# The last job of the first experts taken back tile by tile, and the exact low parts of the second mixer made on VectorE alone

## The chip, the core and the metric

The kernel runs on one core of a Trainium2 chip. The metric is the device time of one launch in microseconds (us), the median of several runs. The core has TensorE (PE, matrix products into PSUM), VectorE (DVE), ScalarE (ACT), GpSimd (POOL), and SyncE (SP), whose queue issues most transfers from HBM. Each engine works through its own list of instructions strictly in the order in which they were written, and waits at an instruction until the semaphores that it names are up.

## What is computed

A first network of two layers (attention and a feed-forward part each) turns 256 tokens of width 1024 into `x`; a second network of two layers follows. Cut to what matters here:

```
for i in range(2):                                   # second network
    hx = modulate(rmsnorm(x, ln1_g[i]), sh1, sc1)     # and hc from ctx
    yx, yc = mixer_ab(...) if i == 0 else mixer_cd(...)
    x = x + g1 * yx
    ...
    out = moe(tokens, ...)        # 32 experts, two per token
    ctx = ctx + g2c * out[:, :n_ctx]                  # layer 0 only
    x = x + g2 * out[:, n_ctx:]
```

The place of interest is the seam between the experts of layer 0 (512 tokens: 256 of `x`, 256 of `ctx`) and the mixer of layer 1 (window attention beside a pooling mixer).

## The kernel before

**Tiles.** The 512 tokens are four tiles of 128, counted `t4` = 0, 1 (of `X`) and 2, 3 (of `C`, the context). A tile's row of 1024 is handled in two halves of 512 columns.

**Experts.** `moe` runs jobs of two experts each. Per job PE multiplies the gathered tokens by gate and up weights (L1973), then the hidden by the down weights (L2017); ACT and DVE split the result `Y` into an exact high and low part (`split_T`, L417 and L418). `combine(t4, halves)` takes a job's result back to a tile: two products on PE (L2026), a multiplication by the gate from PSUM on DVE (L2036, into `tm`), and the addition to the stream, L2038, on GpSimd, or for the last job on DVE. For the last job the first halves of all four tiles are taken back inside `moe`; the second halves come in `tail`, which here is `MixerCD.begin`.

**Exact products.** A matrix product with a fp32 weight is made of three fast ones: `w` is split into `wh` (a copy in the short format, ACT, L300) and `wl` (the rest, a subtraction, L301). `Splits.emit` makes one such chunk of 128x1024; which engine subtracts is its field `engine`:

```
nc.scalar.activation(wh, w, AF.Copy)
self.engine.tensor_tensor(wl, w, wh.bitcast(F32), op=OP.subtract)
```

Tokens are split in the same way in `Normed.finish`: PE turns a tile (L478, eight transposes into two PSUM buffers), ACT scales and shifts the first four pieces (L486) and DVE the last four (L484), ACT copies the high part (L489, twice) and GpSimd subtracts (L490, twice).

**Begin of the second mixer.** `MixerCD.begin` takes the last job back, norms each tile and starts the queries. Per tile, `square` (ACT, L440), `root` (ACT, L386, after which DVE makes the reciprocal root, L397 to L402), `scale` (ACT, L437, half a tile, and DVE, L438, the other half), and `norm.need`, which is `finish`. `queries(t4, ...)` is a product of a tile with four chunks (L319 to L321, twelve matmuls for each half of the depth). `defer(n, f)` calls `f` after `n` ticks of the written order; nothing is decided at run time.

**Run of the second mixer.** `MixerCD.run` makes the queries' rotation (`gqa_q`, from ACT L583 to the transposes L1118 on PE), the keys (L1544), the pooling branch (`U`, copied by ACT at L1569 and used by PE at L1577) and attention units: logits on PE (L1172), row maximum and bias on DVE (L1178), exponentials on ACT (L1190). Chunks for the output product are split meanwhile (L300, L301).

**Order of transfers.** `pump` issues the weights of all stages in one fixed list on SP, one unit of 1 MB per free buffer; a unit's buffer is free when `consumed` is called behind its last reader. So the weights of the second experts (L227, L231) are fetched ahead until the buffers are full, and then follow PE's use of them.

Of the kernel before, what the change touches and what calls it, by code (L numbers as in the profile page):

```python
# [11 lines left out]
F32 = mybir.dt.float32  # L12
# [3 lines left out]
OP = mybir.AluOpType  # L16
# [111 lines left out]
def body(tc, d, dump=None):  # L128
    nc = tc.nc
    es = ExitStack()  # L130
    with es:
# [288 lines left out]
        class Normed:  # L420
# [50 lines left out]
            def finish(self, xn, t4):  # L471
                s, t = TILES[t4]
                ts = slice(t * 128, (t + 1) * 128)
                for k2 in range(2):
                    p = trp().rearrange("p (k t) -> p k t", k=4)
                    for kk in range(4):
                        k = 4 * k2 + kk
                        nc.tensor.transpose(p[:, kk], xn[:, k * 128:(k + 1) * 128], ident)  # L478
                    f = self.whole[s][:, 4 * k2:4 * k2 + 4, ts] if self.whole else self.wk.tile([128, 4, 128], F32, name="spl", bufs=2)
                    for kk in range(4):  # L480
                        k = 4 * k2 + kk
                        sc, sh = scl[:, self.l, 0, s, k:k + 1], modT[:, self.l, 0, k, s:s + 1]
                        if k2:
                            nc.vector.tensor_scalar(f[:, kk], p[:, kk], sc, sh, op0=OP.mult, op1=OP.add)  # L484
                        else:
                            nc.scalar.activation(f[:, kk], p[:, kk], AF.Identity, bias=sh, scale=sc)  # L486
                    if s in self.parts:
                        hi, lo = [h[:, 4 * k2:4 * k2 + 4, ts] for h in self.parts[s]]
                        nc.scalar.activation(hi, f, AF.Copy)  # L489
                        (nc.vector if k2 and t4 in self.ss else nc.gpsimd).tensor_tensor(lo, f, hi.bitcast(F32), op=OP.subtract)  # L490

            def __call__(self, k, t4):
                self.need(t4)
# [950 lines left out]
        class MixerCD:  # L1444
# [10 lines left out]
            def begin(self, combine):  # L1455

                norm, tiles = self.norm, (0, 1, 2, 3)
                there.clear()
                for p in self.rings:
                    del free[p]  # L1460
                norm.whole = [big(n, [128, 8, 256]).bitcast(F32) for n in ("lo0", "lo1")]
                xn = [big(n, [128, 2, D]).bitcast(F32) for n in ("hi0", "hi1")]
                norm.parts = {0: [self.rings[1].tile([128, 2048], F32, name="w").bitcast(F32R).rearrange("p (k t) -> p k t", k=8)
                                  for _ in range(2)]}
                st = {t4: norm.steps(streams[TILES[t4][0]][:, TILES[t4][1]], t4, xn[TILES[t4][0]][:, TILES[t4][1]]) for t4 in tiles}
                square, root, scale = [lambda t4, i=i: st[t4][i]() for i in range(3)]
                sp = self.sp = Splits(self.rings[0], end_moe[0], end_cd, 2, skip=(end_moe[0] + 2,), engine=nc.gpsimd)
                def joined(t4, between=lambda: None):
                    combine(t4)
                    between()  # L1470
                    square(t4)
                    root(t4)

                def one():
                    scale(0)
                    sp.emit()
                    norm.need(0)
                joined(0)
                joined(1, one)
                sp.emit()  # L1480
                scale(1)
                joined(2)
                sp.hold = True
                defer(2, lambda: norm.need(1))
                defer(3, lambda: scale(2))
                self.queries(0, lambda c, t, ps: self.first.append(ps))
                joined(3)
                sp.engine = nc.vector
                self.last = lambda: scale(3)

            def queries(self, t4, done):
# [4 lines left out]
            def run(self, right, more):  # L1496
                norm, sp = self.norm, self.sp
                with ExitStack() as inner:
# [36 lines left out]
                    def keys(tiles, j0):  # L1535

                        ps = []
                        w = units[end_moe[0] + 2]
                        for t4 in tiles:
                            norm.need(t4)  # L1540
                            p = acc()[:, 0:256]
                            s, t = TILES[t4]
                            for k in range(8):
                                nc.tensor.matmul(p, norm.whole[s][:, k, t * 128:(t + 1) * 128], w[:, k], start=k == 0, stop=k == 7)  # L1544
                                if k % 4 == 3:
                                    tick()
                            ps.append(p)
                        sp.hold = False
                        sp.resume(2)
                        if tiles[0] == 2:  # L1550
                            consumed(end_moe[0] + 2)
                            sp.engine = nc.gpsimd
                        gqa_kv(at, ps, tiles, self.tk, KT, V, j0, 5)

                    chain = lambda c, t, ps: gqa_q(at, ps, self.tq, QT, t, 4)
# [48 lines left out]

                    gone = []
                    sp.ended = gone.append
                    sp.engine = nc.vector
                    gated_out(sp, pl, parts, (0, 1), 0, [gate[:, :512]], lambda t4: None, KP)
                    drain()
                    on_tick.remove(beside)  # L1610
# [308 lines left out]
        def moe(l, route, u0, during, ending, tail):  # L1919
# [3 lines left out]
            with ExitStack() as ph:  # L1923
# [259 lines left out]
                jobs = list(range(NE // 2))  # L2183
# [30 lines left out]
                prev = None  # L2214
# [12 lines left out]
                for i, j in enumerate(jobs):  # L2227
                    cur = sides.pop(i)
                    loop = i == OVER + 2
                    if loop:  # L2230
                        tc.mark_branch_hint_location(f"left{l}", engines=[mybir.EngineType.PE])

                    def next_two():
                        sides.update((n, side(jobs[n])) for n in range(i + 1, min(i + 3, len(jobs))))
                        group = Group(list(sides.values())) if sides else None
                        if group:
                            group.match()
                        return group
                    if i % 2 and not loop:
                        group = next_two()  # L2240
                    nxt = sides.get(i + 1)
                    for m in range(2):
                        p = cur.project(m, u)
                        if i == 0 and m == 0:
                            route.weights()
                            cur.turn_P()
                            cur.weights()
                            route.windows(route.rk)
                            if EXTRA[l]:
                                ei, sl, w1 = route.pick(wk, route.none)  # L2250
                                extra.append((sl, w1))
                                wanted[l] = ei
                            route.right.close()
                            wr = ph.enter_context(tc.tile_pool(name=f"wrm{l}", bufs=1, side="right"))
                            gates = [gate_load(wr, l, 1, s) for s in range(NT // 2)]
                        cur.act(m, p)
                        if m == 0 and i + 1 == len(jobs):
                            ending()
                        if prev:
                            for t4 in order if loop and m == 0 else () if loop else order[m * half:(m + 1) * half]:  # L2260
                                prev.combine(t4)
                    cur.hidden_T()
                    if loop:

                        left_over()
                        group = next_two()
                        nxt = sides[i + 1]
                    elif nxt:
                        if i % 2:
                            group.gather()  # L2270
                        nxt.turn_P()
                    for n in range(2):
                        cur.down(n, u)
                        if nxt and n == 0:
                            if loop:
                                group.gather()
                                nxt.turn_P()
                            nxt.weights()
                        if i + 1 == len(jobs) and n:
                            for t4 in range(NT):  # L2280
                                cur.combine(t4, (0,), nc.vector)
                    if i == 0:
                        during()
                    u += cur.units
                    prev = cur
                tail(lambda t4: prev.combine(t4, (1,), nc.vector))

        def put(v, extra=False, whole=False):
            plan.append((v, extra, whole))
# [78 lines left out]
        end_moe = [plan_moe(0)]  # L2368
# [206 lines left out]
```

## Time and profile before

| | |
|---|---|
| median of 3 runs | 2161.28 us (2159.53 to 2161.49) |
| profiled execution, its own time | 2162.79 us |
| span in its profile | 2160.9 us |
| PE busy | 1988.7 us (92%) |
| DVE busy | 1034.2 us (48%) |
| ACT busy | 734.2 us (34%) |
| POOL busy | 398.8 us (18%) |
| SP's transfers, share of 16 DMA engines | 71.5% |
| HBM read | 607.90 MB, 283 GB/s over the span |

Busy shares are averages over very different stages: what bounds the kernel must be read stage by stage. Times in the rows further down are us from the span's start. A wait row names who waited, for whom, and then the total, the number and the longest of the waits. In a timeline row the columns are start, duration, engine, line, operation, what is written and read, the shape, how many were merged, and in brackets the idle time of the engine before it and who ended it.

### The profile page before, as it was taken

Reading aid. Unit: us, or ns where it says so; the run is one execution under the profiler, and the core shown is the slowest. Engines: PE = TensorE matmul, PEld = TensorE weight load, DVE = VectorE, ACT = ScalarE, POOL = GpSimd, SP = SyncE. Lnnn points to the kernel's source line nnn. Section 1 sums busy time; section 2 is a strip of 40 time slices with the busy share of each in tenths; the row PEclk is TensorE's granted clock in tenths of the full one; section 3 lists DMA queues with packets and bytes.
Section 4 is the critical chain, followed back from the end, with each engine's and each line's share of the span. In section 5 each row is a group of like instructions: output and inputs, shape, how many; then the busy total and the mean of one; then the engine's idle time right before and its main releaser. Section 6 shows DMA issues by size and latency. Waiting matters only on the chain. (4 is left out here: it accounts for less than half of the span.)

```text
span 2160.9 us, 28242 instructions
## 1 busy us (share of the span) xinstructions
PE 1988.7 (92%) x10991; PEld 1258.5 (58%) x10991; DVE 1034.2 (48%) x2123; ACT 734.2 (34%) x1287; POOL 398.8 (18%) x353
## 2 busy tenths in 40 slices
PE   7998999998999989677999999999788799998998
PEld 5765888775898878456444454445366444343333
DVE  5745555664667986967423333223553422221222
ACT  5544544555565456353111111111364311111110
POOL 3000110100110100014122333323420111111111
PEclk9999999999999999788999999999999899999999
DMA  9776677665465434105899998999552799999998
GB/s 326 280 253 224 236 254 265 222 251 199 159 203 186 163 119 139 45 25 200 329 421 417 411 412 349 400 413 416 197 205 78 299 420 421 420 421 401 407 421 339
DMA packets 160762, 612.96 MB, mean 284 GB/s; under 512 B 10527, under 2 KB 16255, under 8 KB 111344
## 3 DMA queue, kind: packets, MB, share of 16 engines
q1 hardware_dynamic: 155744, 596.86, 71.5%
q0 software_dynamic: 4448, 13.51, 2.2%
q8 instruction: 88, 1.44, 0.3%
q10 hardware_dynamic: 432, 0.74, 0.1%
q14 instruction: 50, 0.41, 0.1%
HBM read 607.90 MB, written 3.16 MB: 283 GB/s over the span
## 5 line engine op out<-in xcount | busy, mean ns | idle before, releaser
L1973 PE MATMUL acc<-w,XT 128*64 128x512 f32 x1856 | 432.4, 594 | 5.6 <-DMA w<-in_ex_gate_dram 3.4
L301 DVE TENSOR_TENSOR w<-w 128x1024 fp32r<-128x1024 f32 x244 | 297.5, 1231 | 170.2 <-ACT w L300 148.8
L300 ACT ACTIVATE w<-w 128x1024 fp32r<-128x1024 f32 x252 | 264.5, 1059 | 191.4 <-PE acc L321 91.7
L1973 PEld LDWEIGHTS acc<-w,XT 128*64 128x64 f32 x1856 | 136.9, 137 | 265.6 <-issue 239.4
L2036 DVE TENSOR_TENSOR tm<-acc,gate 128x512 f32<-128x512 f32 x196 | 129.5, 686 | 228.3 <-PE acc L2026 177.0
L2017 PE MATMUL acc<-w,hT 128*64 128x512 f32 x912 | 222.7, 613 | 14.0 <-PEq L2191 6.4
L2038 POOL TENSOR_TENSOR X<-X,tm 128x512 f32<-128x512 f32 x124 | 155.3, 1280 | 424.4 <-DVE tm L2036 424.4
L363 PE MATMUL acc<-hi,w 128*128 128x256 f32 x576 | 163.6, 284 | 5.4 <-ACT hi L489 2.2
L364 PE MATMUL acc<-lo,w 128*128 128x256 f32 x576 | 161.7, 281 | 0.8 <-POOL lo L490 0.8
L365 PE MATMUL acc<-hi,w 128*128 128x256 f32 x576 | 161.5, 280 | 0.0
L321 PE MATMUL acc<-w,lo 128*128 128x512 f32 x368 | 149.0, 405 | 1.3 <-POOL lo L1385 1.1
L319 PE MATMUL acc<-w,hi 128*128 128x512 f32 x336 | 141.6, 421 | 6.6 <-ACT hi L1384 5.3
L320 PE MATMUL acc<-w,hi 128*128 128x512 f32 x336 | 135.2, 402 | 8.2 <-DVE w L301 8.2
L2017 PEld LDWEIGHTS acc<-w,hT 128*64 128x64 f32 x912 | 64.1, 139 | 123.6 <-issue 110.5
L1999 ACT ACTIVATE hT<-trp 128x512 f32<-128x512 f32 (+1 forms) x33 | 19.5, 591 | 332.1 <-PE trp L1996 332.1
L2038 POOL TENSOR_TENSOR C<-C,tm 128x512 f32<-128x512 f32 x64 | 79.5, 1273 | 267.7 <-DVE tm L2036 267.7
L1990 DVE SCALAR_TENSOR_TENSOR hd<-sg,ws,acc 128x512 f32<-128x512 f32 (+1 forms) x33 | 36.3, 1099 | 168.7 <-issue 95.2
L363 PEld LDWEIGHTS acc<-hi,w 128*128 128x128 f32 x576 | 108.7, 189 | 7.9 <-ACT hi L489 2.6
L2154 PE MATMUL acc<-P,hi 128*128 128x256 f32 x544 | 103.5, 288 | 8.8 <-issue 6.5
L365 PEld LDWEIGHTS acc<-hi,w 128*128 128x128 f32 x576 | 110.1, 191 | 0.0
L364 PEld LDWEIGHTS acc<-lo,w 128*128 128x128 f32 x576 | 108.8, 189 | 1.5 <-POOL lo L490 1.1
L1317 DVE SCALAR_TENSOR_TENSOR cy<-GT,cols,cy 128x256 f32<-128x256 f32 x240 | 106.9, 502 | 0.3
(423 smaller groups left out, 3359.4 us busy)
## 6 DMA issues: line engine op xcount, KB each, us to landing
w<-in_ex_gate_dram SPq DMA_DIRECT2D x118, 1024.0 KB, 12.5
w<-in_ex_up_dram SPq DMA_DIRECT2D x118, 1024.0 KB, 13.6
w<-in_ex_down_dram SPq DMA_DIRECT2D x118, 1024.0 KB, 13.2
w<-in_ffn_w_dram SPq DMA_DIRECT2D x64, 1024.0 KB, 5.3
fw<-in_mod_w_dram SPq DMA_DIRECT2D x48, 1024.0 KB, 7.5
w<-in_a_w_qkv_dram SPq DMA_DIRECT2D x17, 1024.0 KB, 10.8
w<-in_w_in_ab_dram SPq DMA_DIRECT2D x14, 1024.0 KB, 5.2
w<-in_b_w_qkv_dram SPq DMA_DIRECT2D x12, 1024.0 KB, 5.7
```

The lines of the kernel that those rows point to most:

```text
L300: nc.scalar.activation(wh, w, AF.Copy)
L301: self.engine.tensor_tensor(wl, w, wh.bitcast(F32), op=OP.subtract)
L319: nc.tensor.matmul(ps[:, :n], xh, wh, start=first, stop=False)
L320: nc.tensor.matmul(ps[:, :n], xh, wl, start=False, stop=False)
L321: nc.tensor.matmul(ps[:, :n], xl, wh, start=False, stop=last)
L363: nc.tensor.matmul(z, wh[:, js], xh, start=k == 0 and j % 2 == 0, stop=False)
L364: nc.tensor.matmul(z, wh[:, js], xl, start=False, stop=False)
L365: nc.tensor.matmul(z, wl[:, js], xh, start=False, stop=k == 7 and j % 2 == 1)
L1973: nc.tensor.matmul(p[self.rows(a)], self.XT[:, 4 * k0 + k, self.rows(a)], units[v + a][:, k], start=k0 + k == 0, stop=4 * k0 + k == 7)
L2017: nc.tensor.matmul(self.p[c][self.rows(a)], self.hT[:, 2 * n + k, self.rows(a)], units[v + a][:, k, s], start=n + k == 0, stop=n + k == 2)
L2036: nc.vector.tensor_tensor(g, p, gates[s][:, c], op=OP.mult)
L2038: add.tensor_tensor(dst, dst, g, op=OP.add)
```

## The change

In the first experts the last job's first halves are no longer taken back inside `moe`; `joined(t4)` in the mixer's begin takes back both halves of a tile, then squares it. For tile 1 the scaling and turning of tile 0 stand between its two halves, and for tile 2 the scaling of tile 1 does. The first two weight chunks of the mixer are split after tile 0's square and root. All weight splits of the mixer (eight chunks that GpSimd subtracted) and the four token subtractions of tiles 0 and 1 are DVE's.

```diff
-                        (nc.vector if k2 and t4 in self.ss else nc.gpsimd).tensor_tensor(lo, f, hi.bitcast(F32), op=OP.subtract)
+                        (nc.vector if self.whole or k2 and t4 in self.ss else nc.gpsimd).tensor_tensor(lo, f, hi.bitcast(F32), op=OP.subtract)
...
-                sp = self.sp = Splits(self.rings[0], end_moe[0], end_cd, 2, skip=(end_moe[0] + 2,), engine=nc.gpsimd)
+
                 def joined(t4, between=lambda: None):
-                    combine(t4)
+
+                    combine(t4, (0,))
                     between()
+                    combine(t4, (1,))
                     square(t4)
                     root(t4)
...
                 joined(0)
+                sp = self.sp = Splits(self.rings[0], end_moe[0], end_cd, 2, skip=(end_moe[0] + 2,))
                 joined(1, one)
                 sp.emit()
-                scale(1)
-                joined(2)
+                joined(2, lambda: scale(1))
...
                 joined(3)
-                sp.engine = nc.vector
...
                             consumed(end_moe[0] + 2)
-                            sp.engine = nc.gpsimd
...
-                    sp.engine = nc.vector
...
-                        if i + 1 == len(jobs) and n:
+                        if l and i + 1 == len(jobs) and n:
...
-                tail(lambda t4: prev.combine(t4, (1,), nc.vector))
+                tail(lambda t4, halves=(1,): prev.combine(t4, halves, nc.vector))
```

What stands where on an engine moves with it. Lines of the changed kernel behind the edit are one lower, so its L2035 and L2037 are L2036 and L2038 of before. First DVE at the end of the last job, from the first product that comes back; `gate_9370` is the gate of `X`, `gate_9372` that of `C`. Before:

```order
L2036 TENSOR_TENSOR tm<-acc,gate_9370 128x512
L2038 TENSOR_TENSOR X<-X,tm 128x512
L2036 TENSOR_TENSOR tm<-acc,gate_9370 128x512
L2038 TENSOR_TENSOR X<-X,tm 128x512
L2036 TENSOR_TENSOR tm<-acc,gate_9372 128x512
L2038 TENSOR_TENSOR C<-C,tm 128x512
L2036 TENSOR_TENSOR tm<-acc,gate_9372 128x512
L2038 TENSOR_TENSOR C<-C,tm 128x512
L2036 TENSOR_TENSOR tm<-acc,gate_9370 128x512
L2038 TENSOR_TENSOR X<-X,tm 128x512
L2036 TENSOR_TENSOR tm<-acc,gate_9370 128x512
L2038 TENSOR_TENSOR X<-X,tm 128x512
```

And in the changed kernel, the same place as far as tile 0's reciprocal:

```order
L2035 TENSOR_TENSOR tm<-acc,gate_9370 128x512
L2037 TENSOR_TENSOR X<-X,tm 128x512
L2035 TENSOR_TENSOR tm<-acc,gate_9370 128x512
L2037 TENSOR_TENSOR X<-X,tm 128x512
L301 TENSOR_TENSOR w<-w 128x1024 x2
L2035 TENSOR_TENSOR tm<-acc,gate_9370 128x512
L2037 TENSOR_TENSOR X<-X,tm 128x512
L397 RECIPROCAL rstd<-sd 128x1
```

The four pairs ahead of tile 0's second half have become none, and two chunk subtractions and one pair now stand between tile 0's last addition and its reciprocal. Second, DVE between the scaling of tile 0 and that of tile 1 in the changed kernel, where before there were only the four L484:

```order
L301 TENSOR_TENSOR w<-w 128x1024
L490 TENSOR_TENSOR w<-lo,w 128x4x128
L484 TENSOR_SCALAR lo<-trp,scl,modT 128x128 x4
L490 TENSOR_TENSOR w<-lo,w 128x4x128
L2035 TENSOR_TENSOR tm<-acc,gate_9370 128x512
L2037 TENSOR_TENSOR X<-X,tm 128x512
L301 TENSOR_TENSOR w<-w 128x1024
L2035 TENSOR_TENSOR tm<-acc,gate_9372 128x512
L2037 TENSOR_TENSOR C<-C,tm 128x512
L397 RECIPROCAL rstd<-sd 128x1
```

Tile 1's second half, a chunk subtraction and tile 2's first half now all precede tile 1's reciprocal. Third, DVE at the first four attention units of the changed kernel; before, no L301 stood there:

```order
L301 TENSOR_TENSOR w<-w 128x1024 x3
L1178 ISA P,mx<-acc,w,rows 128x512
L1178 ISA mx 128x1
L1185 TENSOR_SCALAR low<-mx 128x1
L1178 ISA P,mx<-acc,w,rows 128x512
L1178 ISA mx 128x1
L1185 TENSOR_SCALAR low<-mx 128x1
L301 TENSOR_TENSOR w<-w 128x1024
L1178 ISA P,mx<-acc,w,rows 128x512
```

Three chunks now precede the first unit and one stands between the second and the third. ACT and PE change only in place: on ACT the first two L300 stand behind tile 0's square and root, and on PE the transposes of tile 0 stand ahead of three of the products that come back, while both products of tile 3 come back behind the queries of tile 0.

## Rows read from the trace of the kernel before

**Rows 1.** Windows: busy of PE, PEld, DVE, ACT, POOL; PE clock, DMA share, GB/s.

```profile
2100.00:2140.00 40.00, 36.62 (x155) 13.47 (x151) 6.59 (x11) 3.26 (x6) 7.50 (x6) 1.00 1.01 418
```

**Rows 2.** SP's own waits from 1500 us on.

```profile
SPq L227 <- PE acc L1973: 42.1, 18, 21.5
```

**Rows 3.** Timeline where the second experts begin, PE and SP.

```profile
1699.65 0.64 PE L1973 MATMUL acc<-C,XT 128*64 128x512 f32 x1
...
1703.33 0.33 SPq L227 DMA_DIRECT2D C<-in_ex_up_dram  x1
```

**Rows 4.** PE's waits between 1540 and 1720 us, the longest.

```profile
PE trp L478 <- ACT hi L437: 11.5, 1, 11.5
```

**Rows 5.** Timeline at the seam, tile 0, all engines.

```profile
1540.64 2.00 ACT L300 ACTIVATE w<-w 128x1024 fp32r<-128x1024 f32 x2
...
1541.38 0.68 DVE L2036 TENSOR_TENSOR tm<-acc,gate 128x512 f32<-128x512 f32 x1
...
1541.77 5.12 POOL L301 TENSOR_TENSOR w<-w 128x1024 fp32r<-128x1024 f32 x2 [5.12 <-ACT w L300]
...
1542.10 2.60 DVE L2038 TENSOR_TENSOR X<-X,tm 128x512 f32<-128x512 f32 x1
...
1545.33 2.12 DVE L2038 TENSOR_TENSOR X<-X,tm 128x512 f32<-128x512 f32 x1
...
1550.73 0.69 DVE L2038 TENSOR_TENSOR X<-X,tm 128x512 f32<-128x512 f32 x1
...
1552.96 0.17 DVE L397 RECIPROCAL rstd<-sd 128x1 f32<-128x1 f32 x1 [0.22 <-ACT sd L386]
...
1553.75 0.72 ACT L437 ACTIVATE hi<-X,rstd 128x512 f32<-128x512 f32 x1 [0.81 <-DVE rstd L402]
...
1554.52 1.97 PE L478 MATMUL trp<-cst,hi 128*128 128x128 f32 x8 [11.47 <-ACT hi L437]
...
1555.68 1.50 ACT L486 ACTIVATE lo<-trp,modT,scl 128x128 f32<-128x128 f32 x4 [0.26 <-PE trp L478]
...
1556.53 1.36 DVE L484 TENSOR_SCALAR lo<-trp,scl,modT 128x128 f32<-128x128 f32 x4 [2.30 <-PE trp L478]
1557.21 1.35 ACT L489 ACTIVATE w<-lo 128x512 fp32r<-128x512 f32 x2
```

**Rows 6.** L301 on DVE, 1500 to 1720 us: ns min/median/max, first and last start, form.

```profile
L301 DVE TENSOR_TENSOR w<-w x8: 1214/1220/1225, 1584.2 to 1663.8; 128x1024 fp32r<-128x1024 f32 x8
```

**Rows 7.** The same of L490 on DVE, in the whole span.

```profile
L490 DVE TENSOR_TENSOR lo<-spl,hi x2: 1340/1340/1341, 802.4 to 805.9; 128x512 fp32r<-128x512 f32 x2
```

**Rows 8.** Timeline, PE turns tile 1 and then tile 2.

```profile
1561.68 1.09 PE L478 MATMUL trp<-cst,hi 128*128 128x128 f32 x8
...
1571.90 1.03 PE L478 MATMUL trp<-cst,hi 128*128 128x128 f32 x8
```

**Rows 9.** Timeline, the queries of tile 0, from ACT to PE.

```profile
1571.76 0.58 ACT L583 ACTIVATE qr<-acc 128x512 f32<-128x512 f32 x1
...
1577.29 0.63 PE L1118 MATMUL trp<-cst,qr 128*128 128x128 f32 x4
```

**Rows 10.** Timeline of ACT at the first attention units.

```profile
1601.53 1.06 ACT L300 ACTIVATE w<-w 128x1024 fp32r<-128x1024 f32 x1 [0.27 <-ACT KT L1148]
...
1605.33 1.04 ACT L300 ACTIVATE w<-w 128x1024 fp32r<-128x1024 f32 x1
...
1608.21 0.59 ACT L1569 ACTIVATE U<-acc 128x512 f32<-128x512 f32 x1
```

**Rows 11.** Timeline of DVE in the same stretch.

```profile
1602.63 0.75 DVE L1178 CUSTOM_DVE_ANT_0 P<-acc,w,rows 128x512 f32<-128x512 f32 x1 [7.36 <-PE acc L1172]
...
1605.18 0.75 DVE L1178 CUSTOM_DVE_ANT_0 P<-acc,w,rows 128x512 f32<-128x512 f32 x1 [0.75 <-PE acc L1172]
```

**Rows 12.** Timeline of PE in the same stretch.

```profile
1605.57 0.60 PE L1577 MATMUL acc<-hi,U 128*128 128x256 f32 x2
...
1608.85 1.22 PE L1577 MATMUL acc<-hi,U 128*128 128x256 f32 x2 [2.68 <-ACT U L1569]
```

## Prediction

> **What bounds the kernel now.** The page's shares say that PE is 92% busy, which is a mean over stages, so the windows come first. Behind the seam, in the second experts, the DMA share is 1.01 at 418 GB/s [rows 1]: there the end is set by how soon the stream of weights gets going and by nothing that PE does later. So the question is what starts that stream. SP's own waits answer it: from 1500 us on its longest, 21.5 us, is for PE's first gate products, L1973 [rows 2]. The timeline shows the first of these at 1699.65 us and SP's next issue at 1703.33 [rows 3], so SP had stood with full buffers since about 1681.8. A product that frees a buffer later lets every later transfer start later, and no slack stands between. What delays the first L1973 by some us therefore delays the end by as many.
>
> Then I ask what sets that moment, and look at the seam. PE's longest wait there is 11.5 us, for ACT's scaling of tile 0 [rows 4], and the timeline of that stretch shows the chain before it: DVE brings back tiles, ACT squares, DVE makes the reciprocal, ACT scales, PE turns [rows 5]. The change works on that chain. It has to be added up tile by tile, since DVE now has all the subtractions of the begin in its one list.
>
> **Unit prices.** All from [rows 5] unless named. A pair (L2036 and L2038) is 0.72 to the start of the addition and 0.69 for one that nothing disturbs: 1.41. From the last addition's end (1550.73 + 0.69 = 1551.42) to the reciprocal is A = 1.54 (square and root). From there to ACT's scaling B = 0.79, to PE's transposes C = 0.77, from these to ACT's L486 D = 1.16, from that to the first L489 E = 1.53. One L489 is 0.68, the four L484 are 1.36. L300 is about 1.0 [rows 10], L301 on DVE 1.22 [rows 6]. L490 on these tiles has no row on DVE. Below, half of an L301 of twice its size is 0.61; above, 1.34 where it was DVE's in another stage [rows 7]. I take 0.69, the undisturbed addition of the same size and nearest in kind, and keep 4 x 0.65 = 2.6 us for the range.
>
> **Tile 0.** The four first pairs, of which two additions took 2.60 and 2.12 beside GpSimd, become one. DVE begins at 1541.38, and two pairs end at 1544.20. Were that all, the reciprocal would stand 7.2 us earlier. But in DVE's order two L301 and tile 1's first pair now precede it. Root ends at 1545.74, and only then does ACT make the first copy, until 1546.75. Two subtractions end at 1549.2, the pair at 1550.6, and with B and C PE turns tile 0 at 1552.15, against 1554.52: **2.4 us gained**.
>
> **Tile 1.** ACT has its first copied half of tile 0 at 1552.15 + D + E + 0.68 = 1555.5. DVE's list reads L490 (to 1556.2), L484 (1557.6), L490 behind the second copy at 1558.25 (1558.95), and only now tile 1's second pair (1560.35). Before, these subtractions were GpSimd's and the pair was done long ago. Root ends at 1561.9. Behind it ACT makes the third copy (1562.9), DVE its subtraction (1564.1) and tile 2's first pair (1565.5), and then the reciprocal that PE waits for. With B and C PE turns tile 1 at 1567.1 instead of 1561.68 [rows 8]: **5.4 us lost**, the gain gone and more.
>
> **Tiles 2 and 3, to the queries' rotation.** The scaling of tile 1 starts on ACT at 1566.3; DVE's half of it is taken as 0.5 (no row; not above ACT's 0.72). Tile 2's second pair ends at 1568.2, root at 1569.75. L486 of tile 1, ACT's next, takes it to 1571.3. Copies, L490, L484, copy, L490 follow as before (0.68, 0.69, 1.36, 0.68, 0.69): 1575.4, and tile 2's transposes stand at 1576.95 against 1571.90 [rows 8]. DVE then has the reciprocal (0.79), its half of the scaling (0.5) and both pairs of tile 3 (2.82): 1579.5. A, B and ACT's 0.72 of tile 3 come before the queries' L583: 1582.55 against 1571.76 [rows 9]. From L583 to the transposes L1118 were 5.53 us, which I keep, since the rotation is the same work: L1118 at 1588.1 against 1577.29, **10.8 us lost**. Before, 5.39 us went from tile 2's transposes to L1118, without a wait of note; counted from 1576.95 PE reaches L1118 at 1582.3 and stands there some 5.8 us. What covered DVE's extra work before was GpSimd's own list; that cover is gone.
>
> **The attention units.** Counted in the time of before. A copy starts at 1601.53 and ends at 1602.59 [rows 10]; its L301 is now DVE's and stands ahead of the first L1178, which came at 1602.63 [rows 11]. DVE had waited 7.36 us there, so the other subtractions are hidden, but this one ends at 1603.8: 1.2 lost. The fourth copy, at 1605.33 and pushed by the later exponentials to some 1606.2, ends near 1607.3; with L301 the third L1178 starts at 1608.5 instead of 1605.18: 3.3. ACT's copy of `U` at 1608.21 stands behind that unit's exponentials, and PE waits for this copy already, 2.68 us [rows 10, 12]. So **3.2 us** more are PE's.
>
> **PE's speed behind waits.** Behind that wait of 2.68 us the same pair of products took 1.22 instead of 0.60 [rows 12]. PE thus runs at half speed for a while behind a wait, and a wait of 5.8 us ahead of L1118 is new. How long such a while would last there no row shows: nothing below, some 3 us above (five such pairs); I take 1.5.
>
> By the Trainium skill ("TensorE: Matmul & The Clock Gate", Part 1), a PE that stood idle comes back at the low one of its two clocks; the halved pair agrees.
>
> **Sum.** 10.8 + 3.2 + 1.5 = 15.5 us. The profiled execution took 2162.79 us, 1.5 above the median, and becomes 2178.3; against the median of 2161.28 it is 2176.8, say 2177.
>
> **Rivals.** *Faster, because GpSimd lets go.* Two additions took 2.60 and 2.12 beside GpSimd's subtractions, 0.69 alone [rows 5]: 1.91 + 1.43 = 3.3 us of tile 0's path come back. If the rest of the seam follows tile 0, the gain is 2.4 (2158.9), and 7.2 (2154.1) if the two L301 move out of its way too. It is decided at tile 1: PE must turn it at or before 1561.68. Against it is DVE's list, where three subtractions and two foreign pairs now precede tile 1's reciprocal.
>
> The Trainium skill has the rule behind this ("SBUF — State Buffer", Who interferes with whom): DVE and GpSimd share a pair of ports under an exclusive lock, and the one that loses stands still. The long additions agree with it; by this rule alone the change would be a gain.
>
> *No change, because the transfers hide it.* The second experts run at the transfers' full rate, so a late seam could be made up: 2161.3. For it speaks the DMA share of 1.01; against it that SP stands 21.5 us with full buffers, ended by PE itself [rows 2, 3]. Nothing can be fetched ahead in that time.
>
> *Slower, but little.* If PE's waits overlap (its wait at the `U` copy may shrink as L1118's grows) and DVE's list is less stiff than added up, tile 1's 5.4 us is what stays: 2166.7.
>
> *Slower still.* The slow clock lasts over the whole stretch of attention, whose products PE then does more slowly between one wait and the next; with L490 at 1.34 us (2.6) and the clock at 3 us and more, 17 + 5 and above: over 2183.
>
> **How the numbers follow.** A change of 0.2%, 4.3 us, is about what can be told from none here. The forecast, a loss between 8 and 22 us, gets 0.80: it rests on sums of measured rows and on fixed lists. Faster 0.05, no change 0.04, the small loss 0.06, over 22 us 0.05. Below, the rotation's 10.8 without attention and clock gives 2172, and 2 to 3 less where waits overlap: 2169. Above, 2.6 for L490 and 1.5 more of the clock give 2181, with 2 for a loss of the same kind in the attention units: 2183. Outside lie the other cases, about 0.16 by their chances, and the ends of the forecast case. Faster 0.05, same 0.04, slower 0.91.
>
> **What would show it.** In the changed profile tile 0's transposes should start near 1552, tile 1's near 1567, tile 2's near 1577, L1118 near 1588 behind a PE wait for ACT of several us that was not there. L301 should be DVE's alone, at about 1.2 us, GpSimd's busy time lower, and the additions of tile 0 all near 0.69. The first L1178 should be about 12 us later, the third about 14, the first L1973 near 1715, and SP's wait for it longer by the same; behind it the DMA share unchanged. The prediction is wrong if tile 1's transposes come before 1562, if L1118 starts without a wait, or if L1973 is late and the end is not: then SP's buffers had slack that the waits don't show.

## The result and the profile after

The changed kernel takes 2175.25 us (median of 4 runs, 2172.06 to 2177.96), the kernel before 2161.24 beside it (2159.53 to 2161.49). The ratio is 1.0066, its 95% interval 1.0052 to 1.0081. That is 14.0 us slower, where 15.5 were forecast.

The page of the changed kernel gives its span, then busy time, share and number of instructions of each engine:

```profile
span 2174.3 us, 28225 instructions
...
PE 1995.8 (92%) x10991; PEld 1265.0 (58%) x10991; DVE 1041.3 (48%) x2135; ACT 735.2 (34%) x1287; POOL 374.4 (17%) x341
```

DVE did only 7 us more in all and POOL 24 us less. No share hints at a loss; it is one of place. The profiled execution took 2176.66 us, 13.9 more than the one before, and its span is 13.4 us longer. The two executions already differ ahead of the seam: the last split of `Y`, L418, starts at 1539.76 us here and at 1540.78 before, so from there on the changed kernel loses 14.4 us. All shifts below are counted from that L418. First PE, by its timeline through the seam (start, duration, idle time ahead and who ended it; L1545 is L1544 of before):

```profile
1550.85 1.97 PE L478 MATMUL trp<-cst,hi 128*128 128x128 f32 x8 [9.38 <-ACT hi L437]
...
1565.40 1.97 PE L478 MATMUL trp<-cst,hi 128*128 128x128 f32 x8 [7.58 <-ACT hi L437]
...
1574.87 1.10 PE L478 MATMUL trp<-cst,hi 128*128 128x128 f32 x8 [0.54 <-ACT hi L437]
...
1585.86 1.09 PE L1118 MATMUL trp<-cst,qr 128*128 128x128 f32 x4 [5.42 <-issue]
1586.74 2.85 PE L1545 MATMUL acc<-w,lo 128*128 128x256 f32 x8
1589.43 1.04 PE L478 MATMUL trp<-cst,hi 128*128 128x128 f32 x8
```

Tile 0's transposes are 11.09 us behind L418 instead of 13.74 [rows 5], a gain of 2.65. Tile 1's are 25.64 behind it instead of 20.90 [rows 8], a loss of 4.74, and PE, which had no wait there, now has one of 7.58. Tile 2's are 3.99 late, and L1118 9.59 [rows 9], behind a new wait of 5.42. DVE's timeline says why:

```profile
1539.76 0.69 DVE L418 TENSOR_TENSOR Yl<-acc,Yh 128x512 fp32r<-128x512 f32 x1 [1.05 <-ACT Yh L417]
...
1541.08 0.69 DVE L2037 TENSOR_TENSOR X<-X,tm 128x512 f32<-128x512 f32 x1
1541.69 0.68 DVE L2035 TENSOR_TENSOR tm<-acc,gate 128x512 f32<-128x512 f32 x1
1542.41 0.69 DVE L2037 TENSOR_TENSOR X<-X,tm 128x512 f32<-128x512 f32 x1
1545.70 2.36 DVE L301 TENSOR_TENSOR w<-w 128x1024 fp32r<-128x1024 f32 x2 [2.60 <-ACT w L300]
...
1554.21 0.69 DVE L490 TENSOR_TENSOR w<-lo,w 128x512 fp32r<-128x512 f32 x1 [1.21 <-ACT w L489]
1554.82 1.36 DVE L484 TENSOR_SCALAR lo<-trp,scl,modT 128x128 f32<-128x128 f32 x4
1556.88 0.69 DVE L490 TENSOR_TENSOR w<-lo,w 128x512 fp32r<-128x512 f32 x1 [0.70 <-ACT w L489]
1557.49 0.68 DVE L2035 TENSOR_TENSOR tm<-acc,gate 128x512 f32<-128x512 f32 x1
1558.21 0.69 DVE L2037 TENSOR_TENSOR X<-X,tm 128x512 f32<-128x512 f32 x1
1561.38 1.23 DVE L301 TENSOR_TENSOR w<-w 128x1024 fp32r<-128x1024 f32 x1 [2.49 <-ACT w L300]
```

Ahead of tile 0's second pair (1541.69) stands one pair now, its own first; the section on the change says none, the prediction counts it. The subtractions are short, but DVE stands idle ahead of nearly each of them, for ACT's copy: 2.60, 1.21, 0.70, 2.49 us. Tile 1's second pair, whose product PE had ended at 1553.7, stands at 1557.49 behind two of these waits. At the attention units DVE and then PE show:

```profile
1612.54 1.22 DVE L301 TENSOR_TENSOR w<-w 128x1024 fp32r<-128x1024 f32 x1 [0.36 <-ACT w L300]
1613.68 0.74 DVE L1178 CUSTOM_DVE_ANT_0 P<-acc,w,rows 128x512 f32<-128x512 f32 x1
...
1617.30 1.23 DVE L301 TENSOR_TENSOR w<-w 128x1024 fp32r<-128x1024 f32 x1 [1.83 <-ACT w L300]
1618.44 0.74 DVE L1178 CUSTOM_DVE_ANT_0 P<-acc,w,rows 128x512 f32<-128x512 f32 x1
```
```profile
1622.11 1.22 PE L1577 MATMUL acc<-hi,U 128*128 128x256 f32 x2 [5.49 <-ACT U L1569]
```

The third L1178 and PE's second pair on `U` are both 14.28 us late [rows 11, 12], and the wait of 2.68 has become 5.49. From there the loss passes almost unchanged to the end in this pair of profiles. SP's waits and its timeline, and a window of the second experts (busy of PE, PEld, DVE, ACT, POOL; clock, DMA share, GB/s):

```profile
SPq L227 <- DVE mx L1178: 42.5, 1, 42.5
SPq L227 <- PE acc L1972: 39.1, 17, 21.8
```
```profile
1694.51 0.42 SPq L227 DMA_DIRECT2D lo<-in_ex_up_dram  x1
1716.80 0.33 SPq L227 DMA_DIRECT2D C<-in_ex_up_dram  x1
```
```profile
2110.00:2150.00 40.00, 37.48 (x161) 13.55 (x159) 7.71 (x13) 3.86 (x7) 6.38 (x6) 1.00 1.01 421
```

SP's issue that had been at 1703.33 [rows 3] comes at 1716.80, 14.49 late by the same count, and the rate behind it is that of before [rows 1].

### The profile page after: what moved, and what is told of

Its sections match the earlier page's. It is cut to its first block, busy times and chain, and to the rows that moved or that the text cites. A ratio compares the mean times of both kernels' runs of the same rounds, so it can differ in the third digit from the quotient of the medians.

```text
span 2174.3 us, 28225 instructions
## 1 busy us (share of the span) xinstructions
PE 1995.8 (92%) x10991; PEld 1265.0 (58%) x10991; DVE 1041.3 (48%) x2135; ACT 735.2 (34%) x1287; POOL 374.4 (17%) x341
## 5 line engine op out<-in xcount | busy, mean ns | idle before, releaser
L301 DVE TENSOR_TENSOR w<-w 128x1024 fp32r<-128x1024 f32 x252 | 308.4, 1236 | 184.9 <-ACT w L300 163.4
L300 ACT ACTIVATE w<-w 128x1024 fp32r<-128x1024 f32 x252 | 264.5, 1059 | 193.9 <-PE acc L321 93.4
L2035 DVE TENSOR_TENSOR tm<-acc,gate 128x512 f32<-128x512 f32 x196 | 129.5, 685 | 235.4 <-PE acc L2025 184.3
L2037 POOL TENSOR_TENSOR X<-X,tm 128x512 f32<-128x512 f32 x124 | 155.2, 1279 | 424.3 <-DVE tm L2035 424.3
L2016 PE MATMUL acc<-w,hT 128*64 128x512 f32 x912 | 216.6, 602 | 8.5 <-ACT hT L1998 5.8
L2037 POOL TENSOR_TENSOR C<-C,tm 128x512 f32<-128x512 f32 x64 | 79.5, 1273 | 266.3 <-DVE tm L2035 266.3
## 6 DMA issues: line engine op xcount, KB each, us to landing
w<-in_ex_up_dram SPq DMA_DIRECT2D x118, 1024.0 KB, 14.4
```

The lines of the kernel that those rows point to most:

```text
L2016: nc.tensor.matmul(self.p[c][self.rows(a)], self.hT[:, 2 * n + k, self.rows(a)], units[v + a][:, k, s], start=n + k == 0, stop=n + k == 2)
L2035: nc.vector.tensor_tensor(g, p, gates[s][:, c], op=OP.mult)
L2037: add.tensor_tensor(dst, dst, g, op=OP.add)
```

## The experiments

**Theory.** Each subtraction that is moved to DVE waits for a copy of ACT, and DVE's list is strictly in order, so it makes the next tile's pairs and the row maxima wait too. **Rivals:** the tile-by-tile order itself does it, with another tile's work between a tile's halves; or DVE simply has too much to do; or sharing with GpSimd costs as much as it relieves.

The table holds all runs. Shifts are those of one profile, in us against the kernel before: the start of the row less the start of the last L418, less the same before (tile 0 13.74, tile 1 20.90, L1118 36.51, third L1178 64.40, SP's issue 162.55, end 620.12 behind L418). Ratios are to the kernel before.

| kernel | tile 0 | tile 1 | L1118 | third L1178 | SP's issue | end | ratio (95%) |
|---|---|---|---|---|---|---|---|
| changed | -2.65 | +4.74 | +9.59 | +14.28 | +14.49 | +14.42 | 1.0066 (1.0052 to 1.0081) |
| order_only | -6.22 | -1.13 | -0.03 | -0.06 | -1.60 | -1.78 | 0.9989 (0.9974 to 1.0004) |
| engines_only | -1.05 | +2.82 | +6.30 | +11.09 | +11.36 | +11.20 | 1.0061 (1.0037 to 1.0085) |
| keys_gpsimd | -2.64 | +4.74 | +9.55 | +10.99 | +10.75 | +10.70 | 1.0039 (1.0025 to 1.0053) |
| tokens_gpsimd | -2.65 | +1.94 | +4.57 | +9.59 | +8.45 | +8.41 | 1.0031 (1.0019 to 1.0043) |
| low_later | -2.63 | +1.47 | +6.29 | +11.69 | +9.19 | +9.26 | 1.0042 (1.0027 to 1.0056) |
| begin_gpsimd | -6.21 | -0.18 | +5.93 | +11.63 | +10.21 | +10.20 | 1.0051 (1.0036 to 1.0065) |
| rotation_first | -6.21 | -1.14 | -0.67 | -0.67 | -2.01 | -1.97 | 0.9995 (0.9985 to 1.0004) |
| square_later | -6.22 | -1.12 | -0.27 | -0.27 | -1.66 | -1.62 | 0.9996 (0.9987 to 1.0005) |
| tokens_first | -6.22 | -0.91 | +1.24 | +2.91 | +1.55 | +1.57 | 1.0010 (1.0001 to 1.0019) |

**The two halves of the change.** `order_only` is the changed kernel with its engine edits undone; `engines_only` is the kernel before with only these made:

```diff
-    (nc.vector if self.whole or k2 and t4 in self.ss else nc.gpsimd).tensor_tensor(lo, f, hi.bitcast(F32), op=OP.subtract)
+    (nc.vector if k2 and t4 in self.ss else nc.gpsimd).tensor_tensor(lo, f, hi.bitcast(F32), op=OP.subtract)
...
-    sp = self.sp = Splits(self.rings[0], end_moe[0], end_cd, 2, skip=(end_moe[0] + 2,))
+    sp = self.sp = Splits(self.rings[0], end_moe[0], end_cd, 2, skip=(end_moe[0] + 2,), engine=nc.gpsimd)
...
     joined(3)
+    sp.engine = nc.vector
...
     consumed(end_moe[0] + 2)
+    sp.engine = nc.gpsimd
...
     sp.ended = gone.append
+    sp.engine = nc.vector
```

> The tile-by-tile order of the change alone, every subtraction on the engine of the kernel before. Theory (the loss comes from the subtractions that stand in DVE's list, the order by itself frees tile 0): tile 0's transposes near 1549 to 1551, tile 1's no later than the 1561.7 of before, L1118 one to three us earlier than 1577.3, time 2157 to 2161 us. Rival (the order itself does it, since work of the tile before now stands between a tile's two halves): tile 1's transposes at 1565 or later and 2168 us or more.

> The order of the kernel before, all subtractions of the second mixer on DVE. Theory: tile 0 gains little, the rows of L301 and L490 that stand ahead of the next tile's additions make L1118 some 7 us late, the attention units add 3.3, together 2170 to 2173 us. Rival (the order does it): at most the 3.3 of the attention units, 2164 to 2165 us.

The engines are the loss (+11.2 us at the end), and the order is not: alone it loses nothing at any row of the table. So the rival of the order falls. The halves are no sum in the seam, though: at L1118 -0.03 and +6.30 stand against +9.59 together, at the third L1178 -0.06 and +11.09 against +14.28. The order puts tile 1's second pair behind tile 0's L490; with GpSimd these hold nobody up on DVE, with DVE they do. `engines_only` came near its numbers up to the third L1178, but its median of 5 is 2175.45 us beside 2163.68 of the kernel before, above the 2170 to 2173 expected. Its profile is of the fastest of these executions (2170.15). In time it can't be told from the changed kernel (ratios 1.0061 and 1.0066): the 3 us that the order adds to the engines are shown in the seam alone.

The rows of the seam repeat well: tile 1 is 4.74 late in both kernels that have the same begin, the changed one and `keys_gpsimd`. Behind it, from the third L1178 to SP's issue, the eleven profiles took 95.65 to 98.42 us at a granted clock of 0.86 to 0.89. So the last two columns of the table hold differences of up to 2.8 us that don't come from the seam.

One number missed: in `order_only` L1118 came no earlier. Of the 6.22 us that tile 0 gained, 1.13 is left at tile 1. PE's waits and DVE's and POOL's timelines there:

```profile
PE acc L321 <- POOL w L490: 3.0, 2, 2.4
PE trp L1118 <- issue: 2.8, 1, 2.8
```
```profile
1550.39 2.06 DVE L2040 TENSOR_TENSOR X<-X,tm 128x512 f32<-128x512 f32 x1
...
1554.13 0.13 DVE L390 TENSOR_SCALAR nv<-ss 128x1 f32<-128x1 f32 x1
1554.24 1.05 DVE L400 TENSOR_TENSOR sd<-rstd 128x1 f32<-128x1 f32 x1
1555.32 2.30 DVE L401 SCALAR_TENSOR_TENSOR sd<-sd,nv 128x1 f32<-128x1 f32 x1
1557.66 0.16 DVE L402 SCALAR_TENSOR_TENSOR rstd<-sd,rstd 128x1 f32<-128x1 f32 x1
```
```profile
1551.86 3.41 POOL L490 TENSOR_TENSOR w<-lo,w 128x512 fp32r<-128x512 f32 x2
1555.23 2.38 POOL L301 TENSOR_TENSOR w<-w 128x1024 fp32r<-128x1024 f32 x1
```

Beside GpSimd's subtractions DVE's steps take long, even those on 128 numbers: L401 ends when GpSimd's L301 does, 2.30 us where L402 takes 0.16. L2040, L400 and L401 stand on tile 1's way to its transposes and together take 4.4 us more than undisturbed (0.69, 0.16, 0.16), of the 5.1 that are lost between the two tiles. And L1118 waits 2.8 us for a rotation that stands behind tile 3 on ACT and DVE.

**The parts of the engine change.** Each kernel undoes one of the edits of the diff above in the changed kernel: the chunks from the keys on (its last two lines), the tokens (its first two), or the begin's four chunks (`Splits` with GpSimd, and DVE behind `joined(3)`).

> The changed kernel, but the weight chunks from the keys to the output product are GpSimd's again, as before. Theory: L1118 stays late by 9 to 10 us, and the first and the third L1178 both come 10 to 11 us later than before instead of 11.1 and 13.3; time 2171 to 2173 us against 2175. Rival (the copy of U waits for something other than these subtractions): no difference from the changed kernel, 2175.

> The changed kernel, but the four L490 of tiles 0 and 1 are GpSimd's again, as before. Theory (an L490 in DVE's list holds what stands behind it until ACT has copied, so it costs its wait and not its 0.69 us): tile 1's transposes come 2 to 3 us earlier than in the changed kernel, L1118 some 6 earlier, time 2167 to 2170 us. Rival (only DVE's busy time counts): at most 4 x 0.69 = 2.8 us come back, 2172.5 or more.

> The changed kernel, but the four weight chunks of the begin are GpSimd's again; tokens and later chunks stay on DVE. Theory: tile 0's transposes come as early as with the order alone (3.5 us ahead of the changed kernel), tile 1's 5 to 7 earlier than in the changed kernel, L1118 still 4 to 5 later than before since the L490 remain in DVE's list, and the attention units add their 3.3 us: 2168 to 2171 us. Rival (sharing with GpSimd slows DVE's additions by as much as its list is relieved): 2174 or more.

`keys_gpsimd` is as the theory has it: PE's second L1118, the first L1178 and the third are all 10.99 us late, so nothing is lost between them and the attention's 3.3 us are gone. The row of the third:

```profile
1619.97 0.75 DVE L1178 CUSTOM_DVE_ANT_0 P<-acc,w,rows 128x512 f32<-128x512 f32 x1 [0.75 <-PE acc L1172]
```

It waits for PE again, as before [rows 11], and not for a subtraction. `tokens_gpsimd` gives 2.80 us back at tile 1 and 5.0 at L1118 (6 were expected), more than the 2.8 us that four L490 keep DVE busy. Its median was 2170.19, just above the upper edge. `begin_gpsimd` gives tile 0 3.56 and tile 1 4.92 us back, a hair under the 5 expected; L1118 stays 5.93 late, 1 to 2 more than expected, and the time was 2171.97, also 1 us above. At the third L1178 it is 2.65 us earlier than the changed kernel, so GpSimd's subtractions relieve DVE's list by more than their sharing costs; its ratio, 1.0051 against 1.0066, doesn't tell the two apart. No part alone is the loss: at the third L1178 they give 3.3, 4.7 and 2.7 us back, of the 14.3 that lie between the changed kernel and `order_only`.

**The place in the list.** The same instructions on the same engines, and two of them moved:

```diff
-    (nc.vector if self.whole or k2 and t4 in self.ss else nc.gpsimd).tensor_tensor(lo, f, hi.bitcast(F32), op=OP.subtract)
+    if self.whole and t4 == 0:
+        self.low.append(lambda lo=lo, f=f, hi=hi: nc.vector.tensor_tensor(lo, f, hi.bitcast(F32), op=OP.subtract))
+    else:
+        (nc.vector if self.whole or k2 and t4 in self.ss else nc.gpsimd).tensor_tensor(lo, f, hi.bitcast(F32), op=OP.subtract)
...
+    norm.low = []
     joined(1, one)
+    for f in norm.low:
+        f()
```

> The changed kernel with the same instructions on the same engines; only the two L490 of tile 0 stand behind tile 1's second addition in DVE's list instead of ahead of it. Theory (it is the place in the in-order list that costs, since an L490 makes all behind it wait for ACT's copy): tile 1's transposes come 2.5 to 3 us earlier than in the changed kernel, the first product of the second experts 2 to 4 earlier, time 2171 to 2173 us. Rival (DVE simply has too much to do): no more than 0.5 us, 2175.

DVE's timeline of this run (L2041, L2043 and L491 are L2035, L2037 and L490 of the changed kernel):

```profile
1552.70 1.36 DVE L484 TENSOR_SCALAR lo<-trp,scl,modT 128x128 f32<-128x128 f32 x4
1553.97 0.68 DVE L2041 TENSOR_TENSOR tm<-acc,gate 128x512 f32<-128x512 f32 x1
1554.69 0.69 DVE L2043 TENSOR_TENSOR X<-X,tm 128x512 f32<-128x512 f32 x1
1555.30 1.29 DVE L491 TENSOR_TENSOR w<-lo,w 128x512 fp32r<-128x512 f32 x2
```

No wait is left among these, and tile 1's transposes come 3.27 us earlier than in the changed kernel, at the same amount of work on each engine. Some 1.9 us of it are the two waits that are gone (1.21 and 0.70), 1.2 the time of the two L490, which now lie where DVE would wait for ACT. That it is DVE's amount of work alone falls with it. At the third L1178 2.6 us remain of this gain. At the end it is 5.2, more than expected (the median is 2170.70), and the rest came later, on PE. From its second pair on `U` to SP's issue the two runs have the same long waits of PE but another clock:

```profile
1622.11:1716.80 94.69, 76.83 (x455) 56.06 (x457) 42.03 (x131) 45.24 (x90) 9.27 (x6) 0.87 0.36 136
```
```profile
1618.97:1711.26 92.29, 74.48 (x455) 54.60 (x457) 42.10 (x131) 45.41 (x91) 9.27 (x6) 0.90 0.37 141
```

The first is the changed kernel, the second `low_later`: 2.4 us shorter with a granted clock of 0.90 instead of 0.87, and about as much less of PE's busy time for the same 455 records. `order_only` gained its 1.5 us behind the third L1178 in the same stretch. One profile of each can't say whether that belongs to a kernel or to an execution.

**Towards a faster kernel.** On `order_only` the rotation was written ahead of tile 3's scaling, then tile 3's square was moved behind the rotation too, then GpSimd's L490 of tile 0 went ahead of its third chunk:

```diff
-    self.last()
     Spot(lambda shape: self.hold.tile(shape, F32, name="C"))
     chain(0, 0, self.first[0])
+    self.last()
...
-    joined(3)
+    combine(3, (0, 1))
-    self.last = lambda: scale(3)
+    self.last = lambda: (square(3), root(3), scale(3))
...
     scale(0)
-    sp.emit()
     norm.need(0)
+    sp.emit()
```

> The order of the change with the engines of before, and the rotation of tile 0's queries written ahead of tile 3's scaling. Theory (in the run of the order alone tile 0's queries wait on ACT behind tile 3, whose pairs come back late; PE then stands 2.8 us ahead of L1118): L1118 2 to 3 us earlier than in the order alone, time 0.1 to 0.2 per cent below the kernel before. Rival (tile 3 is then late by as much, and PE waits at its transposes instead): no difference from the order alone.

> As rotation_first, and ACT squares tile 3 only behind the copies that start the rotation. Theory (ACT's and DVE's lists still held the rotation behind tile 3's square and root): PE's wait of 2.2 us ahead of L1118 goes, L1118 comes 2 to 3 us earlier than in the kernel before, time 2157 to 2159 us where before has 2161. Rival (tile 3's transposes are late instead): the first L1178 no earlier than in rotation_first.

> As square_later, and GpSimd's two L490 of tile 0 stand ahead of its third weight chunk. Theory (PE waited 2.4 us for these L490 at the queries of tile 0): the wait shrinks to below 1 us, but tile 1's transposes still wait for ACT, so at most 0.5 us more than square_later. Rival (the later third chunk makes PE wait for L301 instead): no gain or up to 1 us lost against square_later.

All three fell short. `rotation_first` moved L1118 by 0.64 us against `order_only`, not by 2 to 3, and `square_later` by 0.24: PE's wait there stays at 2.2 and 2.5. In `rotation_first` tile 3's root and scaling still lie inside the rotation in DVE's list (from 1567.26 on). So they do in `square_later`, where tile 3's reciprocal waits for ACT, ahead of the rotation's own:

```profile
1569.70 0.17 DVE L390 TENSOR_SCALAR nv<-hss 128x8 f32<-128x8 f32 x1
1571.40 0.16 DVE L397 RECIPROCAL rstd<-sd 128x1 f32<-128x1 f32 x1 [1.53 <-ACT sd L386]
...
1572.59 0.20 DVE L397 RECIPROCAL rstd<-sd 128x8 f32<-128x8 f32 x1
```

`tokens_first` took PE's wait for L490 away, and yet its third L1178 is 2.9 us later than in the kernel before and 3.2 later than in `square_later`. Its DVE and POOL rows:

```profile
1551.98 2.12 DVE L400 TENSOR_TENSOR sd<-rstd 128x1 f32<-128x1 f32 x1
1554.14 2.26 DVE L401 SCALAR_TENSOR_TENSOR sd<-sd,nv 128x1 f32<-128x1 f32 x1
```
```profile
1551.29 5.09 POOL L301 TENSOR_TENSOR w<-w 128x1024 fp32r<-128x1024 f32 x2
```

GpSimd's third and fourth chunk now lie on tile 1's root, where two tiny steps take 4.4 us (0.3 undisturbed, 3.35 in `square_later`). But shorter additions ahead of them make up for most of that, and tile 1's transposes come only 0.2 us later than in `square_later`. The loss is in PE's speed. PE has no wait for L490 now, and stands 5.17 us in one piece ahead of these transposes, where it stood 0.86 in `square_later`. From tile 1's transposes to tile 2's the windows are (busy of PE, PEld, DVE, ACT, POOL; clock, DMA share, GB/s), first `tokens_first`, then `square_later`:

```profile
1557.40:1567.19 9.79, 9.79 (x36) 8.13 (x37) 6.12 (x16) 4.71 (x11) 3.69 (x4) 0.73 0.39 118
```
```profile
1559.98:1568.41 8.43, 7.80 (x37) 6.00 (x38) 7.32 (x16) 4.67 (x11) 3.75 (x4) 1.00 0.34 124
```

That is 1.4 us. From the first L1118 to the second it is 9.93 us at 0.83 against 8.25 at 1.00, another 1.7. What is saved in one wait of PE can thus return as a longer wait and a lower clock behind it. None of the versions is faster than the kernel before by more than its interval.

## Why the prediction held, step by step

**The bound.** The shift at SP's issue went through to the end one to one in every run: the two agree within 0.2 us in the table. That the transfers would hide it is refuted.

**Tiles.** Tile 0: 2.4 forecast, 2.65 measured. Tile 1: 5.4 and 4.74. Tile 2: 5.05 and 3.99. L1118: 10.8 and 9.59. The mechanism is that of the text; the 10.8 of the rotation's term was 1.2 us too large, and 1.06 of this stands already at tile 2. Part of it can be read from DVE's rows: instructions overlap, so that in the changed kernel an addition of 0.69 (1541.08) is followed after 0.61 by the next. I had added full durations, some 0.08 too much at each of the steps that follow on each other.

**The prices** of 0.69 for L490 and 1.22 for L301 were right. What `low_later` and `tokens_gpsimd` add is that the waits ahead of these instructions matter more than their durations (1.9 and 1.2 us of the gain at tile 1 in `low_later`).

**Attention:** 3.2 forecast. From the second L1118 (1595.48, 10.96 late) to the third L1178 it was 3.3, and `keys_gpsimd` took it away.

**PE's speed:** 1.5 forecast. L1118 and the eight L1545 behind the new wait take 3.57 us to the next transposes (1585.86 to 1589.43). In the kernel before the timeline has:

```profile
1577.29 0.63 PE L1118 MATMUL trp<-cst,qr 128*128 128x128 f32 x4
1577.75 1.89 PE L1544 MATMUL acc<-w,lo 128*128 128x256 f32 x8
1579.48 1.04 PE L478 MATMUL trp<-cst,hi 128*128 128x128 f32 x8
```

That is 2.19 us, so 1.38 were lost, and the granted clock shows where: L1118 itself (1.09 us) ran at 0.50, the low level. The windows of these stretches, changed and before:

```profile
1585.86:1589.43 3.57, 3.57 (x13) 3.06 (x14) 3.20 (x11) 0.78 (x2) 0.00 (x0) 0.61 0.02 5
```
```profile
1577.29:1579.48 2.19, 2.19 (x13) 1.94 (x13) 2.00 (x7) 0.49 (x2) 0.00 (x0) 1.00 0.05 15
```

Its size was a pick from between nothing and 3 us, so that it came out is luck. Nor is PE slow behind every wait: in `order_only` L1118 stood 2.78 us, and the same stretch took 2.19 us at 1.00. 9.6 + 1.4 + 3.3 + 0.2 behind the attention units are the 14.5 at SP's issue.

**What was wrong** is the sentence that SP's wait for L1973 would be longer by the same. It is 21.8 us instead of 21.5. Nor was that wait SP's longest from 1500 us on, as the prediction read it: two others were longer. SP's last issue ahead of that wait is late too, at 1694.51 against 1681.38, because buffers for earlier transfers came free later. The wait for an L1178 is 42.5 us here and one for DVE's L1134 32.2, and in the kernel before SP's waits have:

```profile
SPq L227 <- DVE low L1185: 38.6, 1, 38.6
SPq L242 <- DVE hss L1134: 22.8, 1, 22.8
```

These two waits are 3.9 and 9.4 us longer now and have taken up the loss ahead of the last one. The conclusion stood, since SP had full buffers either way. In the chances, the four other cases add up to 0.20, where the prediction has about 0.16, and the 17 + 5 us of its slowest case are not worked out.

**The rival of GpSimd's release** has a true mechanism: without it tile 0's additions take 0.69 each, and in the kernels whose begin is GpSimd's and tile by tile tile 0 gains 6.2 us. But tile 1 decides, as written. By the Trainium skill ("SBUF — State Buffer", Who interferes with whom) a DVE instruction with two inputs in SBUF contends with a GpSimd instruction that reads SBUF, and the later one is blocked until the other ends. The rows of L400 and L401 agree to the tenth of a us (2.30 until GpSimd's end), and so does L390 with one input, 0.13 beside the same GpSimd work.

## What to carry to other kernels

Price an instruction that moves to another engine by what stands behind it in that engine's list while it waits for its input, and not by its duration alone: four subtractions of 0.69 us cost 5 us at L1118. Write an instruction that waits for a third engine behind those whose inputs are ready. And read two parts of a change apart: here the order is harmless on one assignment of engines and costs 3 us in the seam on the other, though the medians don't show these 3 us.

## What the runs showed of the hardware

Beside GpSimd's subtractions not only DVE's large additions grow (2.06 instead of 0.69) but also steps on 128x1: 1.05 to 2.30 us instead of 0.16, while reciprocal and one-input steps keep theirs. The granted clock of PE from the first attention units to the second experts was 0.87 in one execution and 0.90 in another with the same long waits, and that alone is 2.4 us, as much as any gain that was sought here. In the seam, 5.17 us in which PE stood still were followed by transposes at the low one of the clock's two levels (1.97 us, granted 0.50), and two stretches behind them took 3.0 us longer than at the full clock.
